# Attention with a shared bias on one core: bias exponentials cut by q chunks instead of by k blocks

## The chip, the cores and the metric

The kernel runs on one NeuronCore of a Trainium2 chip. The metric is the time of one execution on the device, in microseconds (us). The engines have these names in the profile: PE is TensorE's matmul, PEld its weight load, ACT is ScalarE, DVE is VectorE, POOL is GpSimd and SP is SyncE. Times within a profile are counted from the start of its span, which runs from the program's first instruction to its last.

## The reference

Inputs are q, k and v with 4 batches, 8 heads, 1024 positions and head dimension 64, and one bias of 1024 x 1024 that all 32 heads share.

```python
scale = 1.0 / np.sqrt(head_dim)
scores = scale * np.matmul(q, k.transpose(0, 1, 3, 2))
scores = scores + bias
scores_max = np.max(scores, axis=-1, keepdims=True)
attn = np.exp(scores - scores_max) / (np.sum(np.exp(scores - scores_max), axis=-1, keepdims=True) + 1e-8)
return np.matmul(attn, v).astype(np.float32)
```

## The kernel before

The kernel uses exp(scale·s + bias) = exp(scale·s) · exp(bias), without the maximum. The factor exp(bias) is the same for all heads, so it is computed once, transposed, and kept in SBUF as `eb`. Scores are held transposed: k on the partitions, q along the free dimension.

**Tiling.** The 32 heads form 16 pairs. A *bank* is one PSUM bank of scores: 128 k positions (block kc, 0 to 7) against 512 q positions (half qh, 0 or 1) of one head. There are 512 banks, in the order pair, q half, k block, head. A *score slot* is up to three banks (S0 has one, S1 two, the others three); it fills one of two PSUM buffers of three banks (`ps_s`), which alternate. For each slot TensorE runs `s_fill` (one matmul of 512 columns per bank, L130), ScalarE runs `s_exp` (one exponential of up to 1536 elements per partition, L137, PSUM to the bf16 tile E in SBUF), VectorE multiplies E by `eb` (`mul_pair`, L159 for four banks at a time, L162 for two), and TensorE multiplies E with v (`av_bank`, L187, four matmuls for a bank). v carries a column of ones, so the same product gives the sum for the softmax; VectorE takes its reciprocal (L197) and multiplies (L199), and SP stores. E has six buffers of 12 banks. The last two banks get the bias in another way: TensorE adds it to the scores (L133).

**Loads.** All of q, k, v and bias but the first chunks come by DMAs issued from the POOL queue in program order; they cast float32 to bf16. Position p·8+c lies on partition p as chunk c. Pair 0 is special: its first halves of q and k come by SP and ACT DMAs, the second halves by POOL (`kr0`, L261; `qr0`, L262). The bias is loaded to `btraw`, by chunks of q: chunks 0 to 3 at L263, chunks 4 to 7 at L318, each one DMA of 2 MB in HBM and 1 MB in SBUF. q and k of later pairs come by `load_qk` (L75 for k, L76 for q) and v by `load_v` (L81).

**Transposes.** q and k must be transposed by TensorE. A *piece* (`transpose_pe`, L89) is eight transposes into one of two small PSUM tiles (tags xa and xb of `ps_x`, which the AV sums use too), and a VectorE step: for k a copy (L102), for q a product with a mask that writes both heads' zero-padded versions (L98). The keys of `pieces` are (pair, 1 for k or 0 for q, half). Pair 0's first pieces are written by hand: `q_trans` (L286), and `k_trans` (L281) for k blocks 0 and 1, 2 and 3 (copied at L310) and 4 to 7 (copied at L315).

**Bias slots.** Four bias slots stand between the first score slots. `b_fill` transposes 16 blocks of 128 x 128 of `btraw` (L145) into one of the two `ps_s` buffers, and `b_exp` (L150) writes their exponential to `eb`. Before, a slot (qh, k0) is four k blocks of all four q chunks of a half. The product of a bank (qh, kc) needs `eb[:, qh, kc]`.

**What sets the order.** The first part, to slot 2, is written by hand. The rest is laid out at build time by a planner that simulates three engines with costs (EXP, QK, AV, MUL and so on, in ns) and due times: `bias_at` and `raw_at` are the times at which loads are taken to have landed, `piece_end`, `x_free`, `t_dve` the state that the hand-written part leaves, `eb_at` the time at which a block of `eb` is there. Each engine then runs its instructions in the order in which the planner put them out, and waits on semaphores for what it needs. The list `order` holds all slots; a position in it and `order.insert` set where the bias slots stand, which was S2 to S6, B, S7, B, S8, S9, B, S10, B, S11.

Of the kernel before, what the change touches and what calls it, by code (L numbers as in the profile page):

```python
# [9 lines left out]
BF = mybir.dt.bfloat16  # L10
ACTF = mybir.ActivationFunctionType
# [4 lines left out]
def kernel(  # L16
# [15 lines left out]
    nc = tc.nc  # L32
    B, H, S, D = q.shape
    P = 128
    NCH = S // P
# [3 lines left out]
    HQ = S // 2  # L39
    QC = NCH // 2  # L40
# [5 lines left out]
    bf_ = bias.rearrange("a b (p c) k -> p (a b c) k", p=P)  # L46
# [7 lines left out]
    ps_s = ctx.enter_context(tc.tile_pool(name="ps_s", bufs=2, space=bass.MemoryType.PSUM))  # L54
# [4 lines left out]
    btraw = consts.tile([P, NCH, S], BF)  # L59
    eb = consts.tile([P, 2, NCH, HQ], BF)  # L60
# [11 lines left out]
    def load_qk(pr):  # L72
        qr = raw.tile([P, 2, NCH, D], BF, name="qr")
        kr = raw.tile([P, 2, NCH, D], BF, name="kr")
        nc.gpsimd.dma_start(out=kr.rearrange("p t c d -> p t (c d)"), in_=kf[pr])  # L75
        nc.gpsimd.dma_start(out=qr.rearrange("p t c d -> p t (c d)"), in_=qf[pr])  # L76
        raws[pr] = (qr, kr)

    def load_v(pr):
        for t in range(2):  # L80
            nc.gpsimd.dma_start(out=vall[:, 2 * pr + t, :, :D], in_=vf[pr, :, t])  # L81
# [34 lines left out]
    def e_at(b, n):  # L116
        if b // ET not in etiles:
            etiles[b // ET] = ep.tile([P, ET, HQ], BF, name="E")
        return etiles[b // ET][:, b % ET:b % ET + n, :]

    open_ps = {}

    def s_fill(g):
        if ("S", g) not in open_ps:
            open_ps[("S", g)] = ps_s.tile([P, 3, HQ], F32, tag="s", name="ps")
        ps = open_ps[("S", g)]
        for j, b in enumerate(slots[g]):
            pr, h, qh, kc = banks[b]
            qT, kT = trs[(pr, 0)], trs[(pr, 1)]
            nc.tensor.matmul(ps[:, j, :], kT[:, kc, :], qT[:, h, qh * HQ:(qh + 1) * HQ],  # L130
                             start=True, stop=b not in late_bias)
            if b in late_bias:
                nc.tensor.matmul(ps[:, j, :], ident[:], braw[:, late_bias[b], :], start=False, stop=True)  # L133

    def s_exp(g):
        n = len(slots[g])
        nc.scalar.activation(e_at(slots[g][0], n), open_ps.pop(("S", g))[:, :n, :], ACTF.Exp, scale=scale)  # L137

    def b_fill(qh, k0):

        ps = ps_s.tile([P, 3, 2 * HQ], BF, tag="s", name="pb").rearrange("p b (j q) -> p (b j) q", j=2)
        open_ps[("B", qh, k0)] = ps
        for j in range(4):
            for i in range(QC):
                nc.tensor.transpose(ps[:, j, i * P:(i + 1) * P],  # L145
                                    btraw[:, qh * QC + i, :].rearrange("p (kp kc) -> p kc kp", kc=NCH)[:, k0 + j, :],
                                    ident[:])

    def b_exp(qh, k0):
        nc.scalar.activation(eb[:, qh, k0:k0 + 4, :], open_ps.pop(("B", qh, k0))[:, :4, :], ACTF.Exp)  # L150

    def mul_pair(b, n=2):
        pr, h, qh, kc = banks[b]
# [88 lines left out]
    with tc.manual_schedule():  # L242
# [12 lines left out]
        kT0 = kvp.tile([P, NCH, P], BF, name="kT")  # L255
# [3 lines left out]
        nc.gpsimd.memset(qT0[D:, 0, :HQ], 0.0)  # L259
        nc.gpsimd.memset(qT0[:D, 1, :HQ], 0.0)  # L260
        nc.gpsimd.dma_start(out=kr0[:, :, QC:, :].rearrange("p t c d -> p t (c d)"), in_=kf[0][:, :, QC * D:])  # L261
        nc.gpsimd.dma_start(out=qr0[:, :, QC:, :].rearrange("p t c d -> p t (c d)"), in_=qf[0][:, :, QC * D:])  # L262
        nc.gpsimd.dma_start(out=btraw[:, :QC, :], in_=bf_[:, :QC, :])  # L263
        for x in range(2):
            for y in range(2):
                nc.vector.memset(mask[x * D:(x + 1) * D, y, :], 1.0 if x == y else 0.0)
# [10 lines left out]
        def k_trans(c0, n, tag):  # L277
            px = ps_x.tile([P, n, P], BF, tag=tag, name="px")
            for c in range(n):
                for t in range(2):  # L280
                    nc.tensor.transpose(px[t * D:(t + 1) * D, c, :], kr0[:, t, c0 + c, :], ident[:])  # L281
            return px
# [27 lines left out]
        nc.vector.tensor_copy(kT0[:, 2:QC, :], pk1[:])  # L310
        nc.vector.memset(vall[:, :, :, D:D1], 1.0)
        s_exp(1)
        pk2 = k_trans(QC, QC, "xb")
        s_fill(2)
        nc.vector.tensor_copy(kT0[:, QC:, :], pk2[:])  # L315
        s_exp(2)
        load_v(0)
        nc.gpsimd.dma_start(out=btraw[:, QC:, :], in_=bf_[:, QC:, :])  # L318
        load_qk(1)
        load_v(1)  # L320
        load_qk(2)
# [4 lines left out]
        EXP, EXP0, QK, AV, TP = 427, 62, 216, 170, 350  # L326
        MUL, COPYQ, COPYK, EVAC, SEM = 600, 650, 420, 620, 80
        order = [("S", g) for g in range(3, NS)]
        for at, x in ((4, (0, 0)), (6, (0, 4)), (9, (1, 0)), (11, (1, 4))):
            order.insert(at, ("B",) + x)  # L330
        NO = len(order)
        T0 = 8000.0
        t_act, t_pe, t_dve = T0 + 1400, T0 + 200, T0 + 100
        filled = []
        act_end = []
        x_free = {"xa": T0 - 500, "xb": T0 + 100}
        x_unit = {}
        bias_at = [13300, 20800]
        raw_at = {0: (5900, 7800), 1: (22200, 23500), 2: (26000, 28500)}
        pieces = [(0, 0, 1)]  # L340
        for pr in range(1, NP):
            pieces += [(pr, 1, 0), (pr, 0, 0), (pr, 1, 1), (pr, 0, 1)]

        pieces.append((NP, 0, 0))
        raw_at[NP] = (T0, T0)
        piece_end = {(0, 1, 0): T0, (0, 0, 0): T0, (0, 1, 1): T0 + 200}
        eb_at = {}
        exp_at = {x: T0 + (0 if x < 3 else 1400) for x in range(6)}
        mul_at = {}
# [16 lines left out]
        def pe_cost(t, c):  # L366
            return c * 2 if t < COLD else c
# [5 lines left out]
        def act_end_of(i):  # L373
            if i < 0:
                return T0
            if i < len(act_end):
                return act_end[i]
            return max(t_act, filled[i] + SEM if i < len(filled) else 0) + sum(
                cost_act(j) for j in range(len(act_end), i + 1))

        def pe_fill():
            i = len(filled)
            if i >= NO or i - 2 >= len(act_end):
                return None
            ready = act_end_of(i - 2) + SEM
            item = order[i]
            if item[0] == "S":
                for b in slots[item[1]]:
                    pr, h, qh, kc = banks[b]
                    for key in ((pr, 1, kc // QC), (pr, 0, qh)) + (((NP, 0, 0),) if b in late_bias else ()):  # L390
                        if key not in piece_end:
                            return None
                        ready = max(ready, piece_end[key] + SEM)
                cost = QK * (len(slots[item[1]]) + sum(b in late_bias for b in slots[item[1]]))
            else:
                ready = max(ready, bias_at[item[1]])
                cost = 2 * TP + 250

            def emit(t):
                if item[0] == "S":  # L400
                    s_fill(item[1])
                else:
                    b_fill(item[1], item[2])
                filled.append(t + pe_cost(t, cost))
            return ready, cost, emit
# [163 lines left out]
        def act_pick():  # L569
            i = len(act_end)  # L570
            if i >= len(filled):
                return None
            return max(t_act, filled[i] + SEM), cost_act(i), i

        while len(act_end) < NO or av_next < NA or any(last_left) or dve_q:
            c = []
            a, d, p = act_pick(), dve_pick(), pe_pick()
            if a:
                c.append((a[0], 0))
            if d:  # L580
                c.append((max(t_dve, d[0]), 1))
            if p:
                c.append((p[0], 2))
            if not c:
                p = pe_pick(force=True)
                c.append((p[0], 2))
            t, who = min(c)
            if who == 0:
                i = a[2]
                item = order[i]  # L590
                t_act = t + a[1]
                act_end.append(t_act)
                if item[0] == "S":
                    s_exp(item[1])
                    for b in slots[item[1]]:
                        exp_at[b] = t_act
                        if b in late_bias:
                            mul_at[b] = t_act
                else:
                    b_exp(item[1], item[2])  # L600
                    for kc in range(4):
                        eb_at[(item[1], item[2] + kc)] = t_act
            elif who == 1:
                if d in dve_q:
                    dve_q.remove(d)
                t_dve = t + d[2]
                d[3](t)
            else:
                t_pe = t + pe_cost(t, p[1])
                p[2](t)  # L610
# [30 lines left out]
```

## Time and profile before

| | us |
|---|---|
| median of 4 executions | 250.55 |
| lowest and highest | 250.21, 251.59 |
| the profiled execution | 250.21 |
| its span | 247.9 |
| ScalarE busy in it | 239.9 |
| VectorE busy in it | 220.5 |
| TensorE busy (matmuls) in it | 226.5 |
| mean granted TensorE clock | 0.996 of full speed |

The difference between the time and the span, 2.3 us, lies around the program's instructions. A row of the timeline gives start, duration, engine, line, operation, the tile written and those read, the shape and the count of merged instructions; brackets hold the engine's idle time ahead of it and what ended that. Matmuls are pipelined, so their rows overlap; exponentials on ScalarE overlap by about 0.1 us.

### The profile page before, as it was taken

To read this page: it belongs to the slowest core of one execution; us is meant where nothing else is said; L and a number is where in the kernel's file an instruction comes from. 1 tells how busy PE (TensorE), PEld (TensorE's weight loads), DVE (VectorE), ACT (ScalarE), POOL (GpSimd) and SP (SyncE) were. 2 spreads that over 40 slices of the span, in tenths; PEclk is the share of its full clock that TensorE was granted. 3 is DMA by queue.
4 is the path that set the end of the run, shared out by engine and by line. 5 is a ranking of instruction groups with operands and counts; after the bars stand their busy time and mean duration, and the time that the engine had idled before them with its cause. 6 is when DMAs were issued, how large, how long until landed. Compare 5 with 4: busy or idle time off the path is not lost.

```text
span 247.9 us, 7157 instructions
## 1 busy us (share of the span) xinstructions
PE 226.5 (91%) x3105; PEld 141.2 (57%) x3160; DVE 220.5 (89%) x393; ACT 239.9 (97%) x183; POOL 53.6 (22%) x74
## 2 busy tenths in 40 slices
PE   8768999999999999999999989999999999999893
PEld 4346656566555655656656655565555555665452
DVE  5236999999999999999999999999999999998884
ACT  4999999999999999999999999999999999999993
POOL 6563534204013040315050500501600000000000
PEclk9999999999999999999999999999999999999998
DMA  5999999923934749494949941492791102020112
GB/s 117 188 200 190 200 128 208 93 87 50 162 49 88 84 90 126 87 130 74 141 67 105 150 67 42 66 151 42 128 90 42 45 0 89 3 85 3 52 56 65
DMA packets 48463, 23.79 MB, mean 96 GB/s; under 512 B 34480, under 2 KB 44592, under 8 KB 48176
## 3 DMA queue, kind: packets, MB, share of 16 engines
q0 software_dynamic: 42272, 14.42, 53.5%
q1 hardware_dynamic: 5872, 8.72, 9.8%
q8 instruction: 24, 0.39, 0.7%
q10 hardware_dynamic: 288, 0.20, 0.2%
q14 instruction: 7, 0.06, 0.1%
HBM read 29.36 MB, written 8.39 MB: 152 GB/s over the span
## 4 chain that ended last, share of the span: by engine, by line
ACT 61%; PE 22%; DVE 13%; issue 2%; ACTq 0%
ACT E L137 58%; PE ps L130 13%; PE po L187 5%; DVE E L162 4%; ACT eb L150 3%; DVE E L159 2%; DVE qT L98 2%; PE px L89 2%; DVE oall L199 2%; PE ps L272 1%; DVE E L156 1%; DVE kT L102 1%; DVE rs L197 1%; PE px L281 0%; PE px L286 0%
## 5 line engine op out<-in xcount | busy, mean ns | idle before, releaser
L137 ACT ACTIVATE E<-ps 128x1536 bf16<-128x1536 f32 (+2 forms) x172 | 230.1, 1697 | 1.0 <-PE ps L130 1.0
L130 PE MATMUL ps<-qT,kT 128*128 128x512 bf16 x457 | 134.7, 379 | 11.0 <-ACT E L137 5.5
L187 PEld LDWEIGHTS <-E 128*128 128x128 bf16 x2016 | 81.3, 98 | 40.1 <-DVE E L162 5.1
L187 PE MATMUL po<-vall,E 128*128 128x65 bf16 x2016 | 92.6, 194 | 3.3 <-DVE E L162 1.2
L159 DVE TENSOR_TENSOR E<-E,eb 128x2048 bf16<-128x2048 bf16 x66 | 79.7, 1216 | 6.4 <-ACT eb L150 6.0
L162 DVE TENSOR_TENSOR E<-E,eb 128x1024 bf16<-128x1024 bf16 x116 | 76.5, 683 | 2.7 <-ACT E L137 1.9
L130 PEld LDWEIGHTS <-kT 128*128 128x128 bf16 x512 | 45.3, 97 | 39.8 <-issue 8.6
L75 POOL DMA_DIRECT2D kr<-in_k_dram x15 | 10.5, 700 | 89.5 <-PE px L89 84.3
L81 POOL DMA_DIRECT2D vall<-in_v_dram x32 | 28.1, 883 | 6.4 <-DVE kT L315 4.2
L199 DVE TENSOR_TENSOR oall<-po,rs 128x256 f32<-128x256 f32 x63 | 26.7, 424 | 2.2
L98 DVE TENSOR_TENSOR qT<-px,mask 128x1024 bf16<-128x1024 bf16 x31 | 21.3, 687 | 4.0 <-PE px L89 3.2
L76 POOL DMA_DIRECT2D qr<-in_q_dram x15 | 10.8, 719 | 29.3 <-PE px L89 25.5
L102 DVE COPY kT<-px 128x512 bf16<-128x512 bf16 x30 | 12.6, 420 | 1.8 <-PE px L89 1.3
L89 PE MATMUL px<-ident,qr 128*64 128x128 bf16 x248 | 12.8, 225 | 0.1
L197 DVE RECIPROCAL rs<-po 128x4 f32<-128x4 f32 x63 | 11.1, 176 | 2.0 <-PE po L187 1.7
L89 PEld LDWEIGHTS <-qr 128*64 128x64 bf16 x248 | 8.0, 109 | 8.6 <-issue 5.9
L89 PE MATMUL px<-ident,kr 128*64 128x128 bf16 x240 | 12.4, 224 | 0.1
L89 PEld LDWEIGHTS <-kr 128*64 128x64 bf16 x240 | 7.7, 109 | 7.9 <-issue 3.2
L150 ACT ACTIVATE eb<-pb 128x2048 bf16<-128x2048 bf16 x4 | 7.5, 1882 | 0.0
L145 PE MATMUL pb<-ident,btraw 128*128 128x128 bf16 x64 | 4.6, 225 | 1.6 <-ACT eb L150 1.0
L145 PEld LDWEIGHTS <-btraw 128*128 128x128 bf16 x64 | 4.5, 146 | 2.4 <-issue 1.4
L156 DVE TENSOR_TENSOR E<-E,eb 128x1024 bf16<-128x1024 bf16 (+2 forms) x7 | 4.6, 685 | 0.2 <-ACT E L137 0.2
(44 smaller groups left out, 27.5 us busy)
## 6 DMA issues: line engine op xcount, KB each, us to landing
out_dram<-oall SPq DMA_DIRECT2D x28, 256.0 KB, 2.2
vall<-in_v_dram POOLq DMA_DIRECT2D x32, 128.0 KB, 5.6
kr<-in_k_dram POOLq DMA_DIRECT2D x15, 256.0 KB, 3.8
qr<-in_q_dram POOLq DMA_DIRECT2D x15, 256.0 KB, 5.1
btraw<-in_bias_dram POOLq DMA_DIRECT2D x2, 1024.0 KB, 9.2
out_dram<-oall SPq DMA_DIRECT2D x7, 128.0 KB, 4.0
k0f<-in_k_dram SPq DMA_DIRECT2D x2, 128.0 KB, 3.0
q0f<-in_q_dram ACTq DMA_DIRECT2D x1, 128.0 KB, 2.7
```

What stands on the lines that cost most here:

```text
L81: nc.gpsimd.dma_start(out=vall[:, 2 * pr + t, :, :D], in_=vf[pr, :, t])
L89: nc.tensor.transpose(px[t * D:(t + 1) * D, c, :], src[:, t, half * QC + c, :], ident[:])
L98: nc.vector.tensor_tensor(dst[:, :, half * HQ:(half + 1) * HQ], px.rearrange("p c q -> p (c q)").unsqueeze(1).to_broadcast([P, 2, HQ]), ma ...
L102: nc.vector.tensor_copy(dst[:, half * QC:(half + 1) * QC, :], px[:])
L130: nc.tensor.matmul(ps[:, j, :], kT[:, kc, :], qT[:, h, qh * HQ:(qh + 1) * HQ], start=True, stop=b not in late_bias)
L137: nc.scalar.activation(e_at(slots[g][0], n), open_ps.pop(("S", g))[:, :n, :], ACTF.Exp, scale=scale)
L150: nc.scalar.activation(eb[:, qh, k0:k0 + 4, :], open_ps.pop(("B", qh, k0))[:, :4, :], ACTF.Exp)
L159: nc.vector.tensor_tensor(e, e, eb[:, qh, kc:kc + 2, :].unsqueeze(2).to_broadcast([P, 2, 2, HQ]), op=ALU.mult)
L162: nc.vector.tensor_tensor(e, e, eb[:, qh, kc:kc + 1, :].to_broadcast([P, n, HQ]), op=ALU.mult)
L187: nc.tensor.matmul(acc[:, i, :], e[:, 0, i * P:(i + 1) * P], vall[:, 2 * pr + h, kc, :], start=(kc == 0 and i == 0), stop=(kc == NCH - 1), ...
L197: nc.vector.reciprocal(rs[:], acc[:, :, D:D1])
L199: nc.vector.tensor_tensor(oall[:, c0:c0 + QC, :], acc[:, :, :D], rs[:].to_broadcast([P, QC, D]), op=ALU.mult)
```

## The change

A bias slot (qh, c0) is now two q chunks of all eight k blocks. The transposes are as many and as large, in another order in the PSUM tile; the exponential writes, for each of eight blocks, a run of 256 elements of `eb`. A half of `eb` is complete for a block only with its second slot. The bias is loaded in four DMAs, of two chunks each; the first goes ahead of the second half of pair 0's q in the POOL queue. The first two bias slots stand one place earlier in `order`: S2 to S5, B, S6, B, S7, S8, S9, B, S10, B, S11. The eight transposes of k blocks 4 to 7 of pair 0 stand behind slot 2's matmuls instead of ahead of them, and the copy is cut in a block and three. The planner's due times and the cost of a bias fill are changed with it.

```diff
-    def b_fill(qh, k0):
-
-        ps = ps_s.tile([P, 3, 2 * HQ], BF, tag="s", name="pb").rearrange("p b (j q) -> p (b j) q", j=2)
-        open_ps[("B", qh, k0)] = ps
-        for j in range(4):
-            for i in range(QC):
-                nc.tensor.transpose(ps[:, j, i * P:(i + 1) * P],
-                                    btraw[:, qh * QC + i, :].rearrange("p (kp kc) -> p kc kp", kc=NCH)[:, k0 + j, :],
+    def b_fill(qh, c0):
+
+        ps = ps_s.tile([P, 3, 2 * HQ], BF, tag="s", name="pb").rearrange("p b (k c q) -> p (b k) c q", c=2, q=P)
+        open_ps[("B", qh, c0)] = ps
+        for c in range(2):
+            for kc in range(NCH):
+                nc.tensor.transpose(ps[:, kc, c, :],
+                                    btraw[:, qh * QC + c0 + c, :].rearrange("p (kp kc) -> p kc kp", kc=NCH)[:, kc, :],
                                     ident[:])
 
-    def b_exp(qh, k0):
-        nc.scalar.activation(eb[:, qh, k0:k0 + 4, :], open_ps.pop(("B", qh, k0))[:, :4, :], ACTF.Exp)
+    def b_exp(qh, c0):
+        nc.scalar.activation(eb[:, qh, :, c0 * P:(c0 + 2) * P],
+                             open_ps.pop(("B", qh, c0))[:, :NCH].rearrange("p k c q -> p k (c q)"), ACTF.Exp)
...
         nc.gpsimd.dma_start(out=kr0[:, :, QC:, :].rearrange("p t c d -> p t (c d)"), in_=kf[0][:, :, QC * D:])
+        nc.gpsimd.dma_start(out=btraw[:, :2, :], in_=bf_[:, :2, :])
         nc.gpsimd.dma_start(out=qr0[:, :, QC:, :].rearrange("p t c d -> p t (c d)"), in_=qf[0][:, :, QC * D:])
-        nc.gpsimd.dma_start(out=btraw[:, :QC, :], in_=bf_[:, :QC, :])
+        nc.gpsimd.dma_start(out=btraw[:, 2:QC, :], in_=bf_[:, 2:QC, :])
...
         s_exp(1)
+        s_fill(2)
+        s_exp(2)
         pk2 = k_trans(QC, QC, "xb")
-        s_fill(2)
-        nc.vector.tensor_copy(kT0[:, QC:, :], pk2[:])
-        s_exp(2)
+        nc.vector.tensor_copy(kT0[:, QC:QC + 1, :], pk2[:, :1, :])
+        nc.vector.tensor_copy(kT0[:, QC + 1:, :], pk2[:, 1:, :])
         load_v(0)
-        nc.gpsimd.dma_start(out=btraw[:, QC:, :], in_=bf_[:, QC:, :])
+        for c in (QC, QC + 2):
+            nc.gpsimd.dma_start(out=btraw[:, c:c + 2, :], in_=bf_[:, c:c + 2, :])
...
-        for at, x in ((4, (0, 0)), (6, (0, 4)), (9, (1, 0)), (11, (1, 4))):
+        for at, x in ((3, (0, 0)), (5, (0, 2)), (9, (1, 0)), (11, (1, 2))):
...
-        t_act, t_pe, t_dve = T0 + 1400, T0 + 200, T0 + 100
+        t_act, t_pe, t_dve = T0 + 1400, T0 + 200, T0 + 600
...
-        x_free = {"xa": T0 - 500, "xb": T0 + 100}
+        x_free = {"xa": T0 - 500, "xb": T0 + 600}
...
-        bias_at = [13300, 20800]
-        raw_at = {0: (5900, 7800), 1: (22200, 23500), 2: (26000, 28500)}
+        bias_at = {(0, 0): 10900, (0, 2): 13700, (1, 0): 18600, (1, 2): 20800}
+        raw_at = {0: (5900, 11500), 1: (22200, 23500), 2: (26000, 28500)}
...
-        piece_end = {(0, 1, 0): T0, (0, 0, 0): T0, (0, 1, 1): T0 + 200}
+        piece_end = {(0, 1, 0): T0, (0, 0, 0): T0, (0, 1, 1): T0 + 500}
...
-                ready = max(ready, bias_at[item[1]])
-                cost = 2 * TP + 250
+                ready = max(ready, bias_at[item[1:]])
+                cost = 1000
...
-                    for kc in range(4):
-                        eb_at[(item[1], item[2] + kc)] = t_act
+                    if item[2]:
+                        for kc in range(NCH):
+                            eb_at[(item[1], kc)] = t_act
```

## The prediction

> **What bounds the kernel now.** I read the page's engine line and groups first, then ScalarE's timeline, then the timeline of all engines up to 32 us, the DMA issues, and VectorE by stages. From the page (busy time, share and count of each engine; then ScalarE's two groups):
>
> ```profile
> PE 226.5 (91%) x3105; PEld 141.2 (57%) x3160; DVE 220.5 (89%) x393; ACT 239.9 (97%) x183; POOL 53.6 (22%) x74
> L137 ACT ACTIVATE E<-ps 128x1536 bf16<-128x1536 f32 (+2 forms) x172 | 230.1, 1697 | 1.0 <-PE ps L130 1.0
> L150 ACT ACTIVATE eb<-pb 128x2048 bf16<-128x2048 bf16 x4 | 7.5, 1882 | 0.0
> ```
>
> ScalarE (ACT) is busy 97% of the span, and idle only 1.0 us before all 172 score exponentials. Its timeline (start, duration) shows where the rest lies:
>
> ```profile
> 7.99 6.82 ACT L137 ACTIVATE E<-ps 128x1536 bf16<-128x1536 f32 x5 [0.30 <-PE ps L130]
> 22.35 1.88 ACT L150 ACTIVATE eb<-pb 128x2048 bf16<-128x2048 bf16 x1
> 27.24 215.95 ACT L137 ACTIVATE E<-ps 128x1536 bf16<-128x1536 f32 x161
> 244.04 0.52 ACT L236 ACTIVATE oh<-po,rh 128x64 f32<-128x64 f32 x2 [0.85 <-DVE rh L232]
> ```
>
> From 7.99 to 243.19 ScalarE never waits: 215.95/161 = 1.34 us per exponential. The chain of waits puts 22% of the span on TensorE and 13% on VectorE; beside a ScalarE without holes this means fills that come just in time, not lost time. So the time is a head (to 7.99), an unbroken row of exponentials, and a tail (243.19 to 247.9). An edit gains only in head or tail, and loses only by making a hole in the row.
>
> **The change part by part.** Sg is score slot g, B a bias slot, times are from the span's start. The timeline rows that I use:
>
> ```profile
> 6.55 0.62 PE L281 MATMUL px<-ident,kr 128*64 128x128 bf16 x12
> 7.00 0.29 DVE L310 COPY kT<-px 128x256 bf16<-128x256 bf16 x1 [1.57 <-PE px L281]
> 10.23 0.41 PE L89 MATMUL px<-ident,qr 128*64 128x128 bf16 x8
> 10.68 0.69 DVE L98 TENSOR_TENSOR qT<-px,mask 128x1024 bf16<-128x1024 bf16 x1 [1.99 <-PE px L89]
> 10.83 0.81 PE L130 MATMUL ps<-qT,kT 128*128 128x512 bf16 x3 [0.19 <-ACT E L137]
> 13.52 1.13 PE L145 MATMUL pb<-ident,btraw 128*128 128x128 bf16 x16 [0.54 <-ACT E L137]
> 16.61 2.36 DVE L159 TENSOR_TENSOR E<-E,eb 128x2048 bf16<-128x2048 bf16 x2 [5.24 <-ACT eb L150]
> 23.74 0.41 PE L89 MATMUL px<-ident,qr 128*64 128x128 bf16 x8
> 24.28 1.15 PE L145 MATMUL pb<-ident,btraw 128*128 128x128 bf16 x16
> ```
>
> *Late k transposes behind S2.* Eight of the 12 transposes leave the place ahead of S2's matmuls. It looks like part of the 0.30 us hole at 7.99. But S2's second and third matmul need the 7.00 copy, which ends at 7.29 and waits for the first four transposes alone; those stay. The matmul ahead of them started at 7.11 and takes 0.215 (0.81 less 0.38 pipeline, over two steps), so it was off the array at 7.33, when the copy released the next. Gain about 0; bounds: at best the whole 0.30. Behind S2 the eight end near 8.2. Their copy is now one block, then three: one VectorE instruction more, in time in which VectorE is idle. S3's third matmul, at 8.75 before, needs the one-block copy near 8.5; were it 0.3 late, the fill would still end before S2's exponential (9.44). Cost 0.
>
> *Slot order.* ScalarE runs S2 to S5, B, S6, B, S7 where it ran S2 to S6, B, S7, B. From S8 on the order and the sums agree: 0. The fill of the first B starts when S4's exponential frees its buffer (7.99 + 6.82 - 2x1.34 = 12.13), takes 1.15, ends near 13.3; S5 ends at 13.47. The second: 15.24 to 16.4, needed at 16.58. The same margin of 0.15 as before, where one bias slot of four lost 0.08 (it ended at 22.35 + 1.88 = 24.23, 1.85 behind the slot ahead, not 1.77). Zero, bounds -0.1 to +0.2.
>
> *Bias in pairs of chunks.* 16 transposes and one exponential of 2048 per slot stay. The exponential now writes eight runs of 256 instead of one of 2048. No row has that shape. Below: equal, 1.77 us from end to end. Above: the cast at L294, with two runs, took 0.40 where the unbroken copy of as many elements at L299 took 0.37; if runs made that 0.03, seven more breaks cost 0.24 on each of four, 1.0 in all. I take 0: the cast also read twice the bytes, so the 0.03 need not be the runs', and the row of L150 itself is nearest in work.
>
> *Bias loads of 1 MB.* The POOL queue now has k, first bias pair, q's second half, second pair; later v, then two bias loads before pair 1's k and q. Two issues more, 0.6 us each of POOL, which has time. What matters is landing (the last column, us from issue):
>
> ```profile
> btraw<-in_bias_dram POOLq DMA_DIRECT2D x1, 1024.0 KB, 9.2
> kr<-in_k_dram POOLq DMA_DIRECT2D x1, 128.0 KB, 3.4
> qr<-in_q_dram POOLq DMA_DIRECT2D x1, 128.0 KB, 4.9
> qr<-in_q_dram POOLq DMA_DIRECT2D x1, 256.0 KB, 11.7
> ```
>
> With issues at 2.42, 3.25 and 3.96, k landed at 5.8, q at 8.1, bias at 13.2. The queue is served in order: 2.3 us for q, 5.0 for bias, half of it 2.5. New landings: first bias pair 8.3, q 5.8 + 2.5 + 2.3 = 10.6, second pair 13.2. Needed: bias at 12.17 and 15.3, slack of 2 us or more. TensorE comes to q's transposes behind S5's fill, at 10.83 + 0.65 = 11.48, so 0.9 of slack; and only past 12.0 would they push the bias fill behind them. VectorE's mask product ends 1.15 later (10.23 to 11.37 before), at 12.6; S6 wants it at 13.5. Upper bound: q behind both pairs, 13.2, a hole of 1.2. I take 0.
>
> Here a rule speaks against the change. The Trainium skill, "DMA: Bandwidth & Descriptors", section "Anatomy of one DMA", prices a DMA at about 2.0 us fixed plus its bytes over the bandwidth, so splitting adds 2.0 us twice. By it q lands at 12.6 (a hole of 0.6) and pair 1's q, which landed at 11.72 + 11.7 = 23.4, at 27.4. Its transposes (23.74 before) stand ahead of the last bias slot's fill; that fill would end at 27.4 + 0.3 + 1.15 = 28.9, ScalarE is ready at 25.5: a hole of 3.4. The trace has bias landing 5.0 us behind q for its 2 MB, with no 2 us between neighbours visible; the page itself puts most of the fixed part into completion, which queued transfers overlap. I take the trace: 0, and keep 3.4 for a rival.
>
> *Later eb.* The first half of eb is whole at 18.35; before, half of it came at 16.58, the rest at 19.69. VectorE's first product moves from 16.61 to 18.4, the fourth ends at 23.0, not 22.1: 0.9 behind. The second half comes at 27.3, where one product of 1.13 could run at 25.0. At most 2.0 us of backlog. VectorE by stages (length, busy):
>
> ```profile
> 16.60:30.00 13.40, 11.26 (x16) 1.00 1.45 194
> 30.00:90.00 60.00, 57.68 (x94) 1.00 0.77 105
> 90.00:150.00 60.00, 57.68 (x101) 1.00 0.76 103
> ```
>
> It idles 2.3 us in each 60, so the backlog is gone by about 90 us. Until then products and AV matmuls come later; six E buffers of 12 banks hold 24 slots, 32 us of exponentials, so ScalarE does not run out of room. The planner reads the later eb and puts AV behind it. Fills keep their place. Cost 0; bounds 0 to 1.6 (2.0 less the 0.4 by which a fill, 0.81 after a release every 1.34, is early). The TensorE order of the last 1000 instructions is the same in both kernels, so the tail stays.
>
> Sum: 0 + 0 + 0 + 0 + 0, with up to -0.1 from a bias slot. The profiled execution took 250.21 us: span 247.9 and 2.3 around it; the median is 250.55, 0.34 above. I forecast 250.5.
>
> **The rivals.**
> *Late landing* (slower): each added load delays the queue by its fixed price. Place: pair 1's q transposes, ahead of the last bias fill. The hole is landing minus 24.0, so it decides the sign (over 1.25 us) from 25.3 on, 1.9 later than now. At the full price 250.5 + 3.4 = 253.9. For: a wait in TensorE's order holds fills too. Against: the even spacing of landings. Chance 0.10.
> *VectorE's backlog reaches the fills* (slower): AV matmuls ahead of fills wait for late products. For: VectorE and TensorE have under 5% to spare from 30 us on. Against: before, TensorE waited for products up to 0.95 us at 21.0, and ScalarE saw nothing. At full size 250.5 + 1.6 = 252.1. Chance 0.12, with smaller holes in the first case's range.
> *Strided exponential:* up to 1.0, 251.5; still within 0.5%. Chance 0.06.
> *The head gives all it has* (faster): 0.30 and 0.1, 250.1; still within 0.5%. Chance 0.10. Faster by 1.25 us needs a shorter first 6 us, which no edit touches: 0.04.
> *No change:* 0.58.
>
> **How the numbers follow.** 0.5% is 1.25 us, about what a measurement of this kernel can tell from no change. Slower by more: 0.22 (the two rivals); faster by more: 0.04; within: 0.74. The range starts at 250.0 (all of the head's gain) and goes to 252.1, the backlog at full size; outside are the late landing beyond that and what is faster.
>
> **What would show it.** Right: ScalarE's score row after the last bias slot stays 1.34 us per exponential without idle, first L150 near 13.4, first L159 near 18.4, q's transposes near 11.5 without a DMA wait, L150 near 1.88. Wrong: idle before L137 released by L130 between 13 and 30 us with a DMA wait on TensorE (late landing); the same between 30 and 90 with waits of L187 on VectorE (backlog); a start of S2's exponential well before 7.9 (the head gained).

## The result, and the profile after

The changed kernel took 250.19 us (median of 36 executions), the kernel before 250.84 (57 executions). The ratio is 0.997, 95% interval 0.9959 to 0.9981: about 0.75 us less (0.5 to 1.0; the two medians differ by 0.65). Two more measurements, among the experiments, gave 0.9977 (0.9958 to 0.9996) and 0.9972 (0.9952 to 0.9992). That lies inside the range and within the 0.5% that was forecast as likeliest. But the forecast summed the edits to zero, and this is not zero. The question is where 0.75 us came from.

The page of the kernel after, its engine line and ScalarE's groups:

```profile
PE 225.9 (91%) x3106; PEld 141.4 (57%) x3160; DVE 218.8 (88%) x382; ACT 239.7 (97%) x183; POOL 54.7 (22%) x76
L137 ACT ACTIVATE E<-ps 128x1536 bf16<-128x1536 f32 (+2 forms) x172 | 230.0, 1665 | 0.1
L150 ACT ACTIVATE eb<-pb 128x2048 bf16<-128x2048 bf16 x4 | 7.5, 1884 | 0.0
```

ScalarE's timeline in it (start, duration; merged rows):

```profile
5.42 7.13 ACT L137 ACTIVATE E<-ps 128x512 bf16<-128x512 f32 x6
12.44 1.88 ACT L150 ACTIVATE eb<-pb 128x2048 bf16<-128x2048 bf16 x1
21.34 1.89 ACT L150 ACTIVATE eb<-pb 128x2048 bf16<-128x2048 bf16 x1
26.24 215.96 ACT L137 ACTIVATE E<-ps 128x1536 bf16<-128x1536 f32 x161
243.04 0.52 ACT L237 ACTIVATE oh<-po,rh 128x64 f32<-128x64 f32 x2 [0.84 <-DVE rh L233]
```

The row of 161 is the same to 0.01 us. It starts 1.0 us earlier than in the profile of before (26.24, not 27.24), and yet the span is 247.8 against 247.9: the stretch behind the last exponential is 5.6 us in this execution and was 4.7 in that one. Over the fourteen profiles of this study it ranges from 4.7 to 6.6 us. In all of them the last store is issued 1.35 us behind the last exponential; what varies is its landing, 2.9 to 4.8 us behind it. So the two spans say nothing of the change, and the 1.0 us is not all its own either. The first score matmuls show why. In the profile of before:

```profile
5.16 1.46 PE L130 MATMUL ps<-qT,kT 128*128 128x512 bf16 x3
```

and in that of after:

```profile
4.83 0.98 PE L130 MATMUL ps<-qT,kT 128*128 128x512 bf16 x3
```

The same three matmuls took 1.46 us and 0.98. In the trace of before the record of the full TensorE clock begins at 6.80 us, in that of after at 3.94; and in the twelve traces of the experiments it lies between 3.8 and 5.4 as well. The profile on which the prediction rests is the one with the late clock, and with it the late head. That turns out to matter for more than the head.

To leave head and tail aside I use from here on the *row*: the time from the end of S1's exponential to the end of the last score exponential, and the *holes* in it, a hole being the excess of the time from one exponential's end to the next over the usual 1.343 us (1.771 for a bias slot). Before: row 235.51, holes 0.41 ahead of S2, 0.08 ahead of the third bias slot. After: row 235.27, hole 0.26 ahead of S2.

### The profile page after: what moved, and what is told of

It is laid out like the page before. It is cut to its first block, busy times and chain, and to the rows that moved or that the text cites. A ratio compares the mean times of both kernels' runs of the same rounds, so it can differ in the third digit from the quotient of the medians.

```text
span 247.8 us, 7150 instructions
## 1 busy us (share of the span) xinstructions
PE 225.9 (91%) x3106; PEld 141.4 (57%) x3160; DVE 218.8 (88%) x382; ACT 239.7 (97%) x183; POOL 54.7 (22%) x76
## 4 chain that ended last, share of the span: by engine, by line
ACT 71%; PE 16%; DVE 8%; issue 2%; ACTq 0%
ACT E L137 68%; PE ps L130 11%; ACT eb L150 3%; PE po L188 3%; DVE E L163 2%; DVE E L160 2%; DVE oall L200 1%; DVE E L157 1%; PE ps L274 1%; PE px L89 1%; DVE qT L98 1%; DVE rs L198 0%; DVE kT L102 0%; PE px L288 0%; PE px L283 0%
## 5 line engine op out<-in xcount | busy, mean ns | idle before, releaser
L160 DVE TENSOR_TENSOR E<-E,eb 128x2048 bf16<-128x2048 bf16 x78 | 93.8, 1215 | 5.9 <-ACT eb L150 5.7
L163 DVE TENSOR_TENSOR E<-E,eb 128x1024 bf16<-128x1024 bf16 x92 | 61.0, 683 | 1.9 <-ACT E L137 1.4
L150 ACT ACTIVATE eb<-pb 128x2048 bf16<-128x2048 bf16 x4 | 7.5, 1884 | 0.0
```

The costliest lines, as they stand in the source:

```text
L150: nc.scalar.activation(eb[:, qh, :, c0 * P:(c0 + 2) * P], open_ps.pop(("B", qh, c0))[:, :NCH].rearrange("p k c q -> p k (c q)"), ACTF.Exp)
L160: nc.vector.tensor_tensor(e, e, eb[:, qh, kc:kc + 2, :].unsqueeze(2).to_broadcast([P, 2, 2, HQ]), op=ALU.mult)
L163: nc.vector.tensor_tensor(e, e, eb[:, qh, kc:kc + 1, :].to_broadcast([P, n, HQ]), op=ALU.mult)
```

## The experiments

All are read against the kernel before on the same chip; each ratio has its 95% interval. The interval of one experiment is near ±0.002, or 0.5 us, so the holes in the traces carry more than the ratios do.

**The kernel before against itself.** No edit.

> The kernel before against itself: ratio 1.000; its interval is what this measurement can tell. Its profile is a second sample of the head. Theory A: the second half of k lands after 6.8 us or the full clock comes late, and slot 2 starts late. Theory B: the bias lands after 13.4 us and ScalarE is idle ahead of the first L150.

Ratio 1.0011 (0.9984 to 1.0038). Its second profile is the key to this case. ScalarE's timeline:

```profile
5.90 1.52 ACT L137 ACTIVATE E<-ps 128x512 bf16<-128x512 f32 x2 [0.18 <-PE ps L130]
7.63 6.82 ACT L137 ACTIVATE E<-ps 128x1536 bf16<-128x1536 f32 x5 [0.20 <-PE ps L130]
14.94 1.88 ACT L150 ACTIVATE eb<-pb 128x2048 bf16<-128x2048 bf16 x1 [0.48 <-PE pb L145]
```

and the fill of that slot on TensorE:

```profile
13.70 1.06 PEld L145 LDWEIGHTS <-btraw 128*128 128x128 bf16 x16 [1.57 <-DMA btraw<-in_bias_dram]
```

ScalarE stands idle for 0.48 us at the first bias slot. TensorE's weight loads for the fill stand still for 1.57 us, until the bias landed at 13.66; the PSUM buffer had been free since 13.12. The hole is 0.59 by the measure above. In the first profile the bias landed at 13.17 and S2's exponential started at 7.99, 0.36 later than here. Only there did the landing lie ahead of the need. Theory B is right about this execution; theory A is not: k landed at 5.81, and S2's hole is 0.31.

**The two halves of the change.** The late k transposes alone in the kernel before (with the planner's state for them, not shown):

```diff
+        s_fill(2)
+        s_exp(2)
         pk2 = k_trans(QC, QC, "xb")
-        s_fill(2)
-        nc.vector.tensor_copy(kT0[:, QC:, :], pk2[:])
-        s_exp(2)
+        nc.vector.tensor_copy(kT0[:, QC:QC + 1, :], pk2[:, :1, :])
+        nc.vector.tensor_copy(kT0[:, QC + 1:, :], pk2[:, 1:, :])
```

> The kernel before with the late k transposes alone behind slot 2 (and the planner's state for it). Theory A, that TensorE's wait for the second half of k ahead of slot 2, or its eight transposes at the half clock there, costs the kernel before something in most executions: ratio near 0.997 to 0.998, and ScalarE without a hole between slots 1 and 2. Theory B, that the gain comes from the bias landing earlier: ratio 1.000 within 0.0007.

Ratio 1.0001 (0.998 to 1.0023). The bias landed at 13.51, and the hole is there:

```profile
14.80 1.88 ACT L150 ACTIVATE eb<-pb 128x2048 bf16<-128x2048 bf16 x1 [0.18 <-PE pb L145]
```

S2's hole is 0.31, as in the second profile of before. S3 got one of 0.27, which no other profile has:

```profile
7.94 0.25 PEld L89 LDWEIGHTS <-qr 128*64 128x64 bf16 x8 [0.27 <-DMA qr<-in_q_dram]
9.14 5.48 ACT L137 ACTIVATE E<-ps 128x1536 bf16<-128x1536 f32 x4 [0.16 <-PE ps L130]
```

With the new state the planner put q's transposes ahead of S3's fill, where they waited for q (landed at 7.90); in the kernel before they stand two fills later, at 10.23. So this kernel differs from before by more than the late transposes, and 0.27 us of its row is a cost of that order. This half gives nothing that the ratio can show.

The rest of the change, with the k transposes back ahead of slot 2 (the diff above reversed, in the changed kernel):

> The changed kernel with the late k transposes put back ahead of slot 2: bias slots by chunk pairs and loads of 1 MB alone. Theory A: ratio 1.000 within 0.0007 and a hole of 0.2 to 1.0 us ahead of slot 2's exponential. Theory B, that in many executions of the kernel before its bias lands later than 13.5 us and stalls the first bias slot: ratio near 0.997 to 0.998, no idle ScalarE time at the bias slots.

Ratio 0.9984 (0.9962 to 1.0007): its side is that of theory B, but the interval reaches 1. And its profile is not clean. On TensorE:

```profile
11.57 0.25 PEld L89 LDWEIGHTS <-qr 128*64 128x64 bf16 x8 [1.00 <-DMA qr<-in_q_dram]
```

q's second half landed at 11.53 here, and its transposes stand ahead of the first bias fill. ScalarE idles 0.26 us ahead of the first L150 (hole 0.36). S2 has a longer hole too, 0.47 instead of 0.31:

```profile
7.41 5.48 ACT L137 ACTIVATE E<-ps 128x1536 bf16<-128x1536 f32 x4 [0.36 <-PE ps L130]
```

k's second half landed at 6.16 and held the transposes ahead of S2's matmuls by about 0.15 us: the twelve took 0.70 us here, 0.53 in the second profile of before. That is the wait of theory A, seen in this profile alone, and it is what the late transposes take away.

The whole change beside them:

> The changed kernel again, beside its two halves on one chip: ratio 0.996 to 0.998 if the recorded gain is real; it should equal the product of the ratios of the two halves if they are independent.

Ratio 0.9977 (0.9958 to 0.9996), the product of the halves 0.9985; these agree within their intervals, which are wide. q landed at 11.41, with a hole of 0.19 at the first bias slot.

**The same delay in both kernels.** An unused load of 0.5 MB goes into the POOL queue behind q's second half, ahead of the load that follows it:

```diff
+        nc.gpsimd.dma_start(out=junk[:], in_=bf_[:, 0, :])
         nc.gpsimd.dma_start(out=btraw[:, :QC, :], in_=bf_[:, :QC, :])
```

In the kernel before:

> The kernel before with one unused load of 0.5 MB from HBM queued between q's second half and the first bias load, so the bias lands about 1.3 us later (near 14.9 us) and q as before. Theory B, that the first bias slot waits for this landing in most executions: ScalarE idle ahead of the first L150 of 1.3 to 1.9 us, ratio 1.005 to 1.007. If the landing had been covered as the prediction held for the kernel before: idle time of 1.3 less the 0.3 of slack, 1.0 us, ratio 1.004, while its own executions would show none.

Ratio 1.0073 (1.0047 to 1.01). The bias landed at 15.07. The hole was not the 1.3 to 1.9 expected:

```profile
17.08 1.88 ACT L151 ACTIVATE eb<-pb 128x2048 bf16<-128x2048 bf16 x1 [2.85 <-PE pb L146]
20.91 1.88 ACT L151 ACTIVATE eb<-pb 128x2048 bf16<-128x2048 bf16 x1 [0.61 <-PE pb L146]
```

The fills tell why (TensorE's timeline; the third bias slot follows the first two):

```profile
15.12 1.92 PE L146 MATMUL pb<-ident,btraw 128*128 128x128 bf16 x16 [2.72 <-DMA btraw<-in_bias_dram]
19.01 1.87 PE L146 MATMUL pb<-ident,btraw 128*128 128x128 bf16 x16 [0.69 <-ACT eb L151]
24.24 1.16 PE L146 MATMUL pb<-ident,btraw 128*128 128x128 bf16 x16
```

and the stages (length; busy time of PE, PEld, DVE, ACT and POOL, with counts; granted clock, 1.00 being full; DMA share and GB/s):

```profile
14.00:15.60 1.60, 0.48 (x5) 0.48 (x6) 0.00 (x0) 0.23 (x1) 0.24 (x1) 0.51 2.04 211
15.60:20.90 5.30, 4.62 (x38) 3.59 (x37) 1.91 (x2) 3.22 (x2) 1.88 (x3) 0.50 1.05 203
20.90:30.00 9.10, 7.71 (x116) 5.37 (x113) 6.30 (x10) 9.09 (x6) 3.34 (x5) 1.00 1.55 191
```

While TensorE waited for the bias its clock fell to half, at 14.05 us, and stayed there for 6.8 us. Two bias fills then took 1.9 us each instead of 1.15, and the second slot got a hole too. In this execution the bias came 1.4 us later than in the second profile of before and cost 2.96 + 0.72 - 0.59 = 3.1 us. It was the slowest of its twelve executions; the median of 252.27 is 1.65 above that of the kernel before. Five of the twelve, this one among them, had a mean granted clock of 0.980 to 0.987 and took 252.21 to 254.64 us; the four with 0.997 to 0.999 took 251.54 to 251.88, 0.9 to 1.3 above the median of before. So the 3.1 us go with the fallen clock, and most of the twelve lost less.

In the changed kernel, with the load ahead of the second bias pair:

> The changed kernel with the same unused load in the same place behind q's second half, ahead of the second bias pair, which then lands near 15.2 us. Theory B says that the change pays because its bias has room: idle time ahead of the second L150 of at most 0.3 us, ratio to the kernel before 0.997 to 0.999, against 1.005 to 1.007 for the same load in the kernel before. If both kernels lack room, both lose about 1.3 us.

Ratio 1.0034 (1.0004 to 1.0064), outside what was expected. At the second bias slot there is no hole: the second pair landed at 13.85 us and was not needed before the first slot's exponential was done. The loss is elsewhere:

```profile
22.69 0.25 PEld L90 LDWEIGHTS <-kr 128*64 128x64 bf16 x8 [0.80 <-DMA kr<-in_k_dram]
25.71 1.88 ACT L151 ACTIVATE eb<-pb 128x2048 bf16<-128x2048 bf16 x1 [0.37 <-PE pb L146]
```

Pair 1's k comes later in the same queue, its transposes stand ahead of S10's fill, and the holes are 0.20 at S10 and 0.47 at the last bias slot. This is one load ahead of the place of the prediction's late landing, which was pair 1's q. Pair 1's k landed at 22.65 here and at 21.23 to 21.74 in the changed kernel without the added load, so the room there is near 1 us.

**Only the landing, in the kernel before.** The first bias load is cut behind chunk 2, and the slots of the first half read chunk 2 twice and chunk 3 not at all, so that part of the bias is left out:

```diff
-        nc.gpsimd.dma_start(out=btraw[:, :QC, :], in_=bf_[:, :QC, :])
+        nc.gpsimd.dma_start(out=btraw[:, :QC - 1, :], in_=bf_[:, :QC - 1, :])
+        nc.gpsimd.dma_start(out=btraw[:, QC - 1:QC, :], in_=bf_[:, QC - 1:QC, :])
...
-                                    btraw[:, qh * QC + i, :].rearrange("p (kp kc) -> p kc kp", kc=NCH)[:, k0 + j, :],
+                                    btraw[:, qh * QC + i - (qh == 0 and i == 3), :].rearrange("p (kp kc) -> p kc kp", kc=NCH)[:, k0 + j, :],
```

> The kernel before with its first bias load cut to chunks 0 to 2 (1.5 MB of HBM), chunk 3 as a load of its own behind it, and chunk 2 used twice in the first half's bias slots in place of chunk 3, so that nothing waits for chunk 3: slots, orders and bytes are those of before, only the landing that the first slot waits for is 1.2 us earlier, near 12.2. Theory B: no idle time ahead of the first L150, ratio 0.997 to 0.999. If the gain is not the landing: 1.000 within 0.001 with the hole still there.

Ratio 0.9981 (0.9959 to 1.0004); the interval just reaches 1. The load that the slot waits for landed at 12.81, and the hole is gone with slots and orders as they were:

```profile
7.58 6.82 ACT L137 ACTIVATE E<-ps 128x1536 bf16<-128x1536 f32 x5 [0.20 <-PE ps L130]
14.28 1.90 ACT L150 ACTIVATE eb<-pb 128x2048 bf16<-128x2048 bf16 x1
```

**Only smaller loads, in the kernel before.** The one load becomes two of 1 MB (cut behind chunk 1), the slots stay.

> The kernel before with its first bias load as two loads of 1 MB and the slots as before: each slot still needs all four chunks. Theory B: the second of them lands where the one load landed (13.2 to 13.7), ratio 1.000 within 0.001, hole ahead of the first L150 of landing less 13.2. Rival, that smaller loads are served faster: landing and hole shrink.

Ratio 1.0 (0.9978 to 1.0022). The second load landed at 14.06. The fill ran its first two transposes at 13.16 and then stood still:

```profile
14.10 1.06 PE L145 MATMUL pb<-ident,btraw 128*128 128x128 bf16 x14 [0.66 <-DMA btraw<-in_bias_dram]
15.20 1.88 ACT L150 ACTIVATE eb<-pb 128x2048 bf16<-128x2048 bf16 x1 [0.74 <-PE pb L145]
```

Here loads of 1 MB did not help slots that need both of them.

**Only later slots, in the kernel before.** `order.insert` at 5 and 7 instead of 4 and 6 for the first two bias slots.

> The kernel before with its first two bias slots one place later in the order and nothing else: S2 to S7, B, S8, B. The first bias fill then starts near 14.9 us, behind every bias landing seen so far (13.2 to 13.7). Theory B: no idle time at the bias slots and a ratio of 0.997 to 0.999, as good as the change. Rival, that loads of 1 MB or the chunk pairs give the gain in themselves: 1.000 within 0.001. VectorE's products start 1.3 us later; if that cost anything there would be idle ScalarE time between 20 and 90 us.

Ratio 0.9992 (0.997 to 1.0014). The first bias slot lost its hole, with the bias at 13.38. But the last one got a hole of 0.46: in the order that the planner made from these slots, TensorE waited for pair 1's q right ahead of the last bias fill.

```profile
23.45 0.25 PEld L89 LDWEIGHTS <-qr 128*64 128x64 bf16 x8 [0.57 <-DMA qr<-in_q_dram]
```

So this was not the clean test that I wanted; it moved the wait from one landing to the next.

**q's second half first, in the changed kernel.** The loads of q and of the first bias pair change places again, with `raw_at` 9300 and `bias_at` 11500 for them.

> The changed kernel with q's second half queued ahead of the first bias pair again (q lands near 8.2, the first pair near 11.3, and q's transposes run behind slot 4's fill). In the changed kernel q landed at 10.6 to 11.5 us, and at 11.5 it held the first bias fill by 0.26 us. Theory: no idle time at slots 3 to 7 in any profile, ratio 0.996 to 0.998, at least as good as the changed kernel's 0.9977. Rival: the first bias pair then lands later than its fill can start (11.6 us), and ScalarE idles ahead of the first L150 by landing less 11.6.

Ratio 0.9979 (0.9956 to 1.0002). q landed at 7.73, the first pair at 10.24, the second at 13.02; holes: 0.31 at S2, 0.04 at the last bias slot. Once more, and the changed kernel beside it:

> The changed kernel with q's second half ahead of the first bias pair, again: no hole at slots 3 to 7, ratio 0.996 to 0.998; it should beat the changed kernel on the same chip by up to 0.001 where that one has a hole of 0.2 to 0.3 us at its first bias slot.

> The changed kernel a third time, for its standing beside the kernel with q first: 0.996 to 0.998, with q landing at 10.6 to 11.5 us and a hole of landing less 11.2 at its first bias slot.

Ratios 0.9977 (0.9955 to 1.0) and 0.9972 (0.9952 to 0.9992). With q at 10.19 us the changed kernel had no hole at its first bias slot this time. So putting q first takes away a wait that appeared in some executions, and gives nothing that this measurement sees. No kernel here beats the changed one.

**All profiles together** (us; *ready* is the end of the score exponential ahead of the first bias slot):

| kernel | awaited landing | ready | hole at first bias slot | row |
|---|---|---|---|---|
| before | 13.17 | 14.81 | 0 | 235.51 |
| before, again | 13.66 | 14.46 | 0.59 | 236.01 |
| late k transposes alone | 13.51 | 14.62 | 0.29 | 235.97 |
| 1 MB loads alone | 14.06 | 14.46 | 0.85 | 236.27 |
| later slots alone | 13.38 | 15.57 | 0 | 235.84 |
| before, delayed | 15.07 | 14.23 | 2.96 | 239.07 |
| landing alone | 12.81 | 14.40 | 0 | 235.42 |
| after | q 10.62 | 12.55 | 0 | 235.27 |
| after, again | q 11.41 | 12.95 | 0.19 | 235.51 |
| after, third | q 10.19 | 13.33 | 0 | 235.34 |
| chunk pairs without late k | q 11.53 | 12.89 | 0.36 | 235.85 |
| after, delayed | q 10.02 | 13.12 | 0 | 236.00 |
| q first | 10.24 | 12.76 | 0 | 235.37 |
| q first, again | 10.04 | 12.98 | 0 | 235.14 |

In the kernels with the old slots, the hole follows landing + 1.39 - ready (the fill, and the steps around it). The 1.39 is set by the landing at 13.66. For 13.51 the sum is then 0.28; for 13.17, 12.81 and 13.38 it is negative, and there was no hole. With the loads of 1 MB it gives 0.99 against 0.85, as two of the sixteen transposes had run before; with the delay 2.23 against 2.96, as the clock had fallen.

The mean row of four old-slot profiles that wait for all four chunks (before twice, late k transposes, 1 MB loads) is 235.94, of the changed kernel 235.37: 0.57 us. Of the 0.57, 0.46 lies in the bias slots: the first one's holes average 0.43 against 0.06, and the third's 0.09 is gone; 0.07 is S3's hole in the kernel with the late transposes. Over the two profiles of the kernel before alone the mean is 235.76, so 0.39 us, of which 0.32 lies in the bias slots. The traces show where the gain lies; its size they give only roughly, as 0.3 to 0.5 us in the bias slots.

## Why the prediction was right or wrong

*What bounds the kernel: right.* ScalarE's row of 161 is the same to 0.01 us, and every hole in which the profiles of before and after differ lies in the first 26 us.

*Late k transposes: right at the size 0 for the kernel before, one case missing.* S2's hole is 0.31 in ten of the fourteen profiles, with and without the edit. But those transposes also wait for k's second half. It landed at 5.69 to 5.89 in six of the seven profiles with the old order of loads (6.30 in the other), and at 6.16 to 6.73 in four of the five with the first bias pair right behind it (5.87 in the fifth). At 6.16 it cost 0.15 us with the transposes ahead of S2. In the profile of after it landed at 6.73, when S2's matmuls had been running since 6.06; ahead of them it would have cost more. So the two halves are not independent: the late transposes took no wait out of the kernel before, but covered one that the other half can bring. How often, the profiles are too few to show.

*Slot order and due times: the step that failed.* "The same margin of 0.15 as before" took the kernel before as free of holes at its first bias slot. It compared the margin of the fill, but not that of the landing behind it. The trace even showed the numbers, bias at 13.17 against a fill at 13.52, 0.35 of slack, but the working set landing against need only for the changed kernel. Measured, the slack is gone in most other traces: with the one load the bias lands at 13.38 to 13.66 in three of them, and S2's exponential starts 0.36 to 0.59 us earlier in all six, where TensorE's full clock came at 3.8 to 5.2 us and not at 6.8. The one profile had both the earliest landing and the latest clock. So the term was 0 (bounds -0.1 to +0.2), and it is -0.46 over these few profiles, -0.32 over those of the kernel before alone. The profiled execution took 250.21 us, below the median of 250.84. The rival that would have caught it was missing: that the existing wait is longer in other executions than in the one profiled, and the change takes it away. That 250.19 lies inside the range is in part luck: its lower end was set for gains at the head, which did not come.

*Strided exponential: right.* L150 takes 1884 ns against 1882.

*Loads of 1 MB: right on the whole.* Estimates for the three landings were 8.3, 10.6 and 13.2; measured 9.67, 10.62 and 13.10 in the first profile, up to 10.62, 11.41 and 13.87 in another. Pair 1's q landed at 22.50, not 27.4: the 2.0 us for each added load, weighed there, do not appear. The point from which q's landing decides was set at 12.0; as the row stands earlier than in the profile used, it is near 11.2, and landings at 11.4 and 11.5 cost 0.19 and 0.36 us, where the working took 0. The late landing as a rival has its mechanism shown by the delayed kernel, at pair 1's k, one load ahead of the q that was named; in the three profiles of the change itself it cost nothing.

*Later eb: right.* The first product started at 17.46, four ran without a pause to 22.1, and ScalarE shows no hole behind 26 us. VectorE's stages after (length, busy time; clock and DMA follow):

```profile
16.60:30.00 13.40, 10.65 (x17) 1.00 1.47 197
30.00:90.00 60.00, 58.23 (x93) 1.00 0.89 114
```

It is busier by 0.55 us between 30 and 90, which fits a backlog being worked off. It makes 78 products of four banks instead of 66.

*The signs named ahead.* In the profile of after the first L150 came at 12.44, the first product at 17.46 and q's transposes at 10.66, each about 0.9 us earlier than named, as S2's exponential started at 7.07. q's transposes did wait for their load (10.62), but with room to spare. A start of S2 well before 7.9 had been named as a sign that the head gained. It is not one: S2 starts before 7.9 in every profile but the one behind the prediction, also in the six others with the old slots.

*The head and the tail.* The head that gives all it has was priced at 0.4 us and did not happen. Over seven profiles with the old slots and seven with the new ones, the end of S1's exponential averages 7.38 and 7.28 us, and the stretch behind the last exponential 5.54 and 5.65: no difference clear of their spread. What stays open: 0.3 to 0.4 us of the 0.75 are not assigned to the bias slots.

## What to carry to other kernels

A wait that one profile shows with 0.35 us to spare is not covered: take a second profile of the same kernel, and set each DMA landing against the moment of its need, for the kernel before as much as for the kernel after. Cut a transfer and its consumer alike, so that each piece of work waits for its own piece of data; cutting the transfer alone gave nothing here. When one engine runs without holes, the gain lies at the places where it would first meet a late landing, and a queue that is relieved there shows the next landing behind it.

## What the runs showed of the hardware

The TensorE clock fell to half 1.65 us into a wait of 2.7 us for a load and came back 6.8 us later, so that in this execution a landing 1.4 us later cost 3.1. The full clock began anywhere between 3.8 and 6.8 us of the span, in programs whose first matmul started at 1.07. The same bias load landed at 13.17 and 13.66 us in two executions of one kernel, and q's second half at 10.19 to 11.41 in three of another. k's second half, first in its queue, landed at 5.69 to 5.89 in most profiles with a load of 256 KB of HBM behind it, and at 6.16 to 6.73 in most with one of 1 MB. The stretch from the last exponential to the end of the span took 4.7 to 6.6 us, and the difference was the landing of the last store.
